# The second layer's down projection as seven block products instead of eight, with the sums of weights made by accumulating DMAs

## The chip, the cores and the metric

The kernel runs on one core of one Trainium2 chip. The metric is the device time of one execution in microseconds; the kernel before has a median of 1347.08 us over 3 runs (1346.73 to 1347.09). TensorE is called PE here, VectorE DVE, ScalarE ACT, GpSimd POOL and SyncE SP.

## What is computed

A decoder trunk of two layers over 512 tokens of width 1024: a Mamba-2 mixer and a ConvFFN, then differential attention and a second ConvFFN. The change touches only the last matrix product of the second ConvFFN:

```python
def conv_ffn(x, ln_g, up_w, conv_w, conv_b, down_w):
    u = causal_dwconv(rms_norm(x, ln_g) @ up_w, conv_w, conv_b)
    gate, up = u[..., :FFN_DIM], u[..., FFN_DIM:]
    return (jax.nn.silu(gate) * up) @ down_w
...
    x = x + ff.astype(x.dtype)          # FFN_DIM = 2816, D_MODEL = 1024, SEQ = 512
```

All arrays are float32.

## The kernel before

Every product of float32 operands is made from three matmuls in a fast type: each operand is split into a high part (rounded to float32r by ACT) and a low part (the rest, by DVE), and high times high, high times low and low times high are added in PSUM.

**Weights.** All weights of the program stand in one list, `plan`, in the order in which PE uses them, cut into chunks of 128 partitions by 1024 columns (512 KB). For each chunk `emit_chunk` writes one DMA on SP's queue into a buffer `wr` (three buffers), one ACT instruction that makes `wh` (L147) and one DVE instruction that makes `wl` (L158). `wh` and `wl` have three buffers each. `chunk(key)` hands out the next chunk and emits those up to two places ahead of it.

**The second ConvFFN** (`ffn(1, ...)`) goes over 22 blocks of 128 features, called pairs here since each has a gate and an up product. For a pair, PE makes `ps_g` and `ps_u` (24 matmuls of 128x128 by 128x512 each, `mm3`, L204 to L206), DVE scales them (L931), ACT and DVE make the three taps of the convolution (L932, L934), ACT applies Silu (L995), DVE multiplies gate and up (L1001), and the product is split into `hh` (ACT, L1002) and `hl` (DVE, L1003). The 22 pairs are cut in two parts, 12 and 10. After each part comes its share of the down projection, `down_tokens`: for each half c of the 1024 output columns, four PSUM banks (one for each block of 128 tokens) collect all features of the part. The stationary operand is a block of `hh` or `hl` (features by tokens), the moving one 512 columns of `wh` or `wl` (L970 to L972). At the end of each half, DVE adds the four banks to the residual `xr` (L977, or L983 in the last part, where the halves of 256 columns are stored at once). The last two feature blocks of the very last bank are made in two halves of 256 columns (`end`), so that the last addition is short.

The program is written through a layer that puts the instructions of each engine in an order of its own and sets the waits between them; what that order is for the two kernels is shown below.

Of the kernel before, what the change touches and what calls it, by code (L numbers as in the profile page):

```python
# [18 lines left out]
P = 128  # L19
T = 512  # L20
D = 1024
KB = D // P
NT = T // P
# [5 lines left out]
FFN = 2816  # L29
NPAIR = FFN // P  # L30
HALF = 12
AH = 8
EPS = 1e-6
NEG = -1.0e30
# [5 lines left out]
def trunk_kernel(ctx: ExitStack, tc, x, ssm_ln_g, ssm_in_w, ssm_conv_w, ssm_conv_b, ssm_dt_bias,  # L40
# [46 lines left out]
    out_chunks(NG - 1)  # L87

    def ffn_plan(l):
        for h, (p0, p1) in enumerate(((0, HALF), (HALF, NPAIR))):  # L90
# [97 lines left out]
    def emit_chunk():  # L188
        i = state["next"]
        if i < len(plan):  # L190
            state["next"] = i + 1
            with tc.issue_after(state["rs"]) if i < 5 else nullcontext():
# [715 lines left out]
    def ffn(l, norm, bp, gnext, nnext):  # L908
        with tc.tile_pool(name="ffn_h%d" % l, bufs=1) as hp, tc.tile_pool(name="ffn%d" % l, bufs=1) as fp:
# [13 lines left out]
            def taps(j, p, ps):  # L923
                key = "%s%d_%d" % ("gu"[j], l, p)
                r = rr[0]
                col = lambda t: cf[l][:, 88 * j + 22 * t + p:88 * j + 22 * t + p + 1]
                u = fp.tile([P, T], F32, tag="u", name="u" + key, bufs=3)
                v = fp.tile([P, T], F32, tag="v%d" % j, name="v" + key, bufs=3)
# [3 lines left out]
                act.activation(v, u, AF.Identity, bias=col(3), scale=col(2))  # L932
                for s in range(1, 3):
                    dve.scalar_tensor_tensor(out=v[:, s:], in0=u[:, :T - s], scalar=col(2 - s),  # L934
                                             in1=v[:, s:], op0=ALU.mult, op1=ALU.add)
                return v
# [13 lines left out]
            def down_tokens(p0, n, hh, hl, last):  # L950
                for c in range(2):
                    cols = slice(c * 512, (c + 1) * 512)
                    pss = [mm_bank("ps_d%d_%d_%d" % (p0, c, b)) for b in range(NT)]
                    for k0 in range(0, n, 2):
                        wh, wl = chunk("d%d_%d_%d" % (l, c, p0 + k0))
                        for b in range(NT):
                            ts = slice(b * P, (b + 1) * P)
                            if last and c == 1 and b == NT - 1 and k0 + 2 == n:
                                end = [aux_bank("end%d" % j) for j in range(2)]
                                for j in range(2):  # L960
                                    for k in range(k0, k0 + 2):
                                        h, w = (t[:, k - k0, j * 256:(j + 1) * 256] for t in (wh, wl))
                                        o = end[j][:, :256]
                                        pe.matmul(o, hh[k][:, ts], h, start=k == k0, stop=False)
                                        pe.matmul(o, hh[k][:, ts], w, start=False, stop=False)
                                        pe.matmul(o, hl[k][:, ts], h, start=False, stop=k == n - 1)
                                continue
                            stop = n - 3 if last and c == 1 and b == NT - 1 else n - 1
                            for k in range(k0, k0 + 2):
                                pe.matmul(pss[b], hh[k][:, ts], wh[:, k - k0, :], start=k == 0, stop=False)  # L970
                                pe.matmul(pss[b], hh[k][:, ts], wl[:, k - k0, :], start=False, stop=False)  # L971
                                pe.matmul(pss[b], hl[k][:, ts], wh[:, k - k0, :], start=False, stop=k == stop)  # L972
                            if stop < n - 1 and k0 + 4 == n:
                                dve.tensor_tensor(out=xr[:, b, cols], in0=pss[b], in1=xr[:, b, cols], op=ALU.add)
                    for b in range(NT):
                        if not last:
                            dve.tensor_tensor(out=xr[:, b, cols], in0=pss[b], in1=xr[:, b, cols], op=ALU.add)  # L977
                            continue
                        ended = c == 1 and b == NT - 1
                        for j in range(2):  # L980
                            h = slice(j * 256, (j + 1) * 256)
                            x_ = xr[:, b, c * 512 + j * 256:c * 512 + (j + 1) * 256]
                            dve.tensor_tensor(out=x_, in0=end[j][:, :256] if ended else pss[b][:, h], in1=x_, op=ALU.add)  # L983
                            (act if j != ended else sync).dma_start(
                                out[0, b * P:(b + 1) * P, c * 512 + j * 256:c * 512 + (j + 1) * 256], x_)

            for p0, p1 in ((0, HALF), (HALF, NPAIR)):
                last = p1 == NPAIR
                hh, hl = [], []
                for p in range(p0, p1):  # L990
                    ps = [products(0, p)]
# [6 lines left out]
                    up = taps(1, p, ps[1])  # L998
                    h = hp.tile([P, T], F32R, tag="hh", name="hh%d_%d" % (l, p), bufs=HALF + 1)
                    w = hp.tile([P, T], F32R, tag="hl", name="hl%d_%d" % (l, p), bufs=HALF + 1)  # L1000
                    dve.tensor_tensor(out=ga, in0=ga, in1=up, op=ALU.mult)  # L1001
                    act.activation(h, ga, AF.Copy)  # L1002
                    dve.tensor_tensor(out=w, in0=ga, in1=h.bitcast(F32), op=ALU.subtract)  # L1003
                    hh.append(h)
                    hl.append(w)
                n = p1 - p0
                if nnext is None:
                    down_tokens(p0, n, hh, hl, last)
# [382 lines left out]
```

## Time and profile before

| | |
|---|---|
| median of 3 runs | 1347.08 us (1346.73 to 1347.09) |
| the profiled execution's own time | 1346.85 us |
| its span, first to last instruction | 1345.2 us |
| granted TensorE clock | 1.0 throughout |
| second ConvFFN's first matmul | 977.8 us |
| first share of its down projection | 1113.0 to about 1178.3 us |
| second share | about 1287 to 1341.8 us |

The busy time of an engine is the sum of its instructions' durations. PE's matmuls overlap each other, so PE's busy time says that PE always had one in flight, and the spacing of their starts says how fast it goes. A group of instructions is given by its line, engine and tiles, with its busy time, the mean of one, and the idle time before it with what ended it.

### The profile page before, as it was taken

The page shows a single profiled execution, that of the slowest core. Times are in us where ns is not written, and L with a number is a line of the kernel's source. Part 1 is how long each engine was busy: PE and PEld are TensorE (multiplying, and loading weights), DVE is VectorE, ACT ScalarE, POOL GpSimd, SP SyncE. Part 2 cuts the span into 40 slices and gives each one's busy share as a digit, 9 for nine tenths or more (in the row PEclk, how much of TensorE's full clock was granted, in tenths as well). Part 3 has the DMA queues.
Part 4 walks back from the last instruction along what each step waited for, and adds up shares of the span by engine and source line. Part 5 has one row for each costly group of instructions (what it writes and reads, how often), then busy time and mean ns, then how long its engine had stood idle before and what let it go on. Part 6 is the DMA issues. An engine that isn't in the chain of part 4 may idle for free.

```text
span 1345.2 us, 16977 instructions
## 1 busy us (share of the span) xinstructions
PE 1339.8 (100%) x6461; PEld 1099.9 (82%) x6461; DVE 919.6 (68%) x1540; ACT 644.4 (48%) x1062; POOL 100.3 (7%) x139
## 2 busy tenths in 40 slices
PE   9999999999999999999999999999999999999998
PEld 8878888888888888888888887777888888888887
DVE  7889788788877774367754556778777773367743
ACT  6695653652444442134433556777654442134420
POOL 5330401200110000000002100000100000000000
PEclk9999999999999999999999999999999999999999
DMA  7553433432333332333323422221233333333332
GB/s 205 161 149 95 149 95 116 127 95 70 95 94 95 102 101 94 95 95 99 97 79 109 127 79 93 70 80 49 63 94 94 95 94 94 96 105 97 95 94 78
DMA packets 179826, 135.00 MB, mean 100 GB/s; under 512 B 6492, under 2 KB 163552, under 8 KB 179744
## 3 DMA queue, kind: packets, MB, share of 16 engines
q1 hardware_dynamic: 173872, 120.73, 30.5%
q0 software_dynamic: 4592, 12.08, 2.9%
q8 instruction: 51, 0.84, 0.3%
q10 hardware_dynamic: 1280, 1.10, 0.2%
q14 instruction: 31, 0.25, 0.1%
HBM read 131.64 MB, written 2.25 MB: 100 GB/s over the span
## 4 chain that ended last, share of the span: by engine, by line
PE 97%; DVE 1%; ACT 1%; DMA 0%; issue 0%; SPq 0%
PE ps_g L205 6%; PE ps_u L206 6%; PE ps_g L206 6%; PE ps_u L205 6%; PE ps_u L204 6%; PE ps_g L204 6%; PE ps_in L204 5%; PE ps_in L206 5%; PE ps_in L205 5%; PE ps_d L206 3%; PE ps_d L205 3%; PE ps_d L204 3%; PE ps_d L971 3%; PE ps_d L970 3%; PE ps_d L972 3%; PE ps_o L206 2%
## 5 line engine op out<-in xcount | busy, mean ns | idle before, releaser
L204 PE MATMUL ps_u<-xgh,wh_u 128*128 128x512 f32 x352 | 137.4, 390 | 0.0
L205 PE MATMUL ps_g<-xgl,wh_g 128*128 128x512 f32 x352 | 137.1, 389 | 0.0
L204 PE MATMUL ps_g<-xgh,wh_g 128*128 128x512 f32 x352 | 137.0, 389 | 0.0
L206 PE MATMUL ps_u<-xgh,wl_u 128*128 128x512 f32 x352 | 137.0, 389 | 0.0
L206 PE MATMUL ps_g<-xgh,wl_g 128*128 128x512 f32 x352 | 137.0, 389 | 0.0
L205 PE MATMUL ps_u<-xgl,wh_u 128*128 128x512 f32 x352 | 136.9, 389 | 0.0
L204 PE MATMUL ps_in<-xgh,wh_in 128*128 128x512 f32 x304 | 126.0, 414 | 0.0
L158 DVE TENSOR_TENSOR wl_d<-wr_d,wh_d 128x1024 fp32r<-128x1024 f32 (+1 forms) x46 | 54.2, 1179 | 96.9 <-ACT wh_d L147 96.7
L206 PE MATMUL ps_in<-xgh,wl_in 128*128 128x512 f32 x304 | 119.7, 394 | 0.0
L205 PE MATMUL ps_in<-xgl,wh_in 128*128 128x512 f32 x304 | 119.2, 392 | 0.0
L147 ACT ACTIVATE wh_d<-wr_d 128x1024 fp32r<-128x1024 f32 (+1 forms) x46 | 47.1, 1025 | 130.3 <-PE ps_d L972 62.4
L931 DVE TENSOR_TENSOR uu<-ps_u,nr_f 128x512 f32<-128x512 f32 x44 | 30.4, 691 | 77.6 <-PE ps_u L206 77.6
L1002 ACT ACTIVATE hh<-vg 128x512 fp32r<-128x512 f32 x44 | 27.8, 632 | 114.9 <-DVE vg L1001 114.9
L205 PEld LDWEIGHTS ps_g<-xgl,wh_g 128*128 128x128 f32 x352 | 66.1, 188 | 13.9 <-DVE xgl L479 0.3
L204 PEld LDWEIGHTS ps_g<-xgh,wh_g 128*128 128x128 f32 x352 | 66.2, 188 | 13.8
L206 PEld LDWEIGHTS ps_u<-xgh,wl_u 128*128 128x128 f32 x352 | 66.2, 188 | 13.7
L205 PEld LDWEIGHTS ps_u<-xgl,wh_u 128*128 128x128 f32 x352 | 66.1, 188 | 13.6
L206 PEld LDWEIGHTS ps_g<-xgh,wl_g 128*128 128x128 f32 x352 | 66.0, 188 | 13.6
L204 PEld LDWEIGHTS ps_u<-xgh,wh_u 128*128 128x128 f32 x352 | 66.0, 188 | 13.5
L147 ACT ACTIVATE wh_g<-wr_g 128x1024 fp32r<-128x1024 f32 x44 | 46.7, 1061 | 50.5 <-PE ps_u L205 31.1
L204 PE MATMUL ps_d<-hh,wh_d 128*128 128x512 f32 x176 | 68.5, 389 | 0.0
L205 PE MATMUL ps_d<-hl,wh_d 128*128 128x512 f32 x176 | 68.5, 389 | 0.0
(364 smaller groups left out, 3188.2 us busy)
## 6 DMA issues: line engine op xcount, KB each, us to landing
wr_g<-in_ffn_up_w_dram SPq DMA_DIRECT2D x44, 512.0 KB, 3.8
wr_u<-in_ffn_up_w_dram SPq DMA_DIRECT2D x44, 512.0 KB, 3.9
wr_d<-in_ffn_down_w_dram SPq DMA_DIRECT2D x42, 512.0 KB, 3.7
wr_in<-in_ssm_in_w_dram SPq DMA_DIRECT2D x40, 512.0 KB, 4.0
m<-cumd POOLq DMA_DIRECT2D x16, 512.0 KB, 4.9
wr_out<-in_ssm_out_w_dram SPq DMA_DIRECT2D x16, 512.0 KB, 3.5
wr_k<-in_kv_w_dram SPq DMA_DIRECT2D x8, 512.0 KB, 3.9
wr_q<-in_q_w_dram SPq DMA_DIRECT2D x8, 512.0 KB, 3.8
```

The costliest lines, as they stand in the source:

```text
L147: return act.activation(self.wh[:, :self.n], self.raw[:, :self.n], AF.Copy)
L158: return eng.tensor_tensor(out=self.wl[:, :self.n], in0=self.raw[:, :self.n], in1=self.wh[:, :self.n].bitcast(F32), op=ALU.subtract)
L204: pe.matmul(ps, wh, xh, start=start, stop=False)
L205: pe.matmul(ps, wh, xl, start=False, stop=False)
L206: return pe.matmul(ps, wl, xh, start=False, stop=stop).ins
L931: dve.tensor_tensor(out=u, in0=ps, in1=r, op=ALU.mult)
L970: pe.matmul(pss[b], hh[k][:, ts], wh[:, k - k0, :], start=k == 0, stop=False)
L971: pe.matmul(pss[b], hh[k][:, ts], wl[:, k - k0, :], start=False, stop=False)
L972: pe.matmul(pss[b], hl[k][:, ts], wh[:, k - k0, :], start=False, stop=k == stop)
L1002: act.activation(h, ga, AF.Copy)
```

## The change

The features of a part are taken in twos (even and odd block), the tokens in two halves of 256, the output columns in two halves of 512. That makes the down projection of a part a product of 2x2 blocks with 2x2 blocks, and Strassen's scheme in Winograd's form makes it from seven block products instead of eight. They are made in the order 1, 2, 5, 7, 6, 3, 4 (`SEVEN`).

- **Left operands.** For each two pairs, DVE makes four sums of 128x256 (`sums`, L1011) of the activations, and the seven left operands (three of them plain) are split into `sh` and `sl` (L1014, L1015), in place of `hh` and `hl` of two pairs.
- **Right operands.** `z` is first W00 (product 1), then W01 is added in place (product 5), then W11 (product 6), then W10 (product 4). `x` is W01 + W11 (product 7), `y` is W11 (3), and product 2 reads W10. Each addition is a DMA issued from POOL with `accum_op=ALU.add`, from the weights in DRAM onto the tile in SBUF, once the tile has been split for the product before. `z`, `x` and `y` have two tiles of 128x1024 each, for up to four of a part's twos; `x` and `y` lie in the memory of `xT`, whose last readers are the transposes of `residual`. `ahead` loads `z`, `x` and `y` of a part while its third pair is made; `combine` stands in the place of `Weights.split` in the list of chunks.
- **Results.** Each product has two banks (two blocks of 128 tokens). DVE adds them to `xr`, partly through a running sum `run_sum`: 22 instructions of 128x512 a part, and ACT makes 2 copies.
- **Parts.** The 22 pairs are cut in three parts, 8, 8 and 6 (`PARTS_D`).

```diff
+PARTS_D = (0, 8), (8, 16), (16, 22)
+SEVEN = "1257634"
...
             if l == 1:
-                for c in range(2):
-                    for k in range(p0, p1, 2):
-                        plan.append(("d%d_%d_%d" % (l, c, k), *w_cols(ffn_down_w[l], k, 2, c * 512, 512)))
+                for m in SEVEN:
+                    for q0 in range(0, (p1 - p0) // 2, 2):
+                        plan.append(("s%s_%d_%d" % (m, p0, q0), (m, p0, q0, min(2, (p1 - p0) // 2 - q0))))
                 continue
...
+            def plus(t, p0, q0, nq, j, i):
+                pool.dma_start(view(t, nq), source(p0, q0, nq, j, i), accum_op=ALU.add)
+            def ahead(p0, n):
+                for q0 in range(0, n // 2, 2):
+                    c, nq = q0 // 2, min(2, n // 2 - q0)
+                    for k, j, i in ("z", 0, 0), ("x", 0, 1), ("y", 1, 1):
+                        sync.dma_start(view(raws[k][c], nq), source(p0, q0, nq, j, i))
+                    plus(raws["x"][c], p0, q0, nq, 1, 1)
+            def combine(key, m, p0, q0, nq):
+                c, n = q0 // 2, nq * 512
+                if m == "2":
+                    t = wrp.tile([P, 1024], F32, tag="raw", name="wr_" + key)
+                    sync.dma_start(view(t, nq), source(p0, q0, nq, 1, 0))
+                else:
+                    t = raws["x" if m == "7" else "y" if m == "3" else "z"][c]
...
+                act.activation(wh[:, :n], t[:, :n], AF.Copy)
+                dve.tensor_tensor(out=wl[:, :n], in0=t[:, :n], in1=wh[:, :n].bitcast(F32), op=ALU.subtract)
+                ready.append((key, view(wh, nq), view(wl, nq)))
+                if m in "156":
+                    plus(t, p0, q0, nq, *{"1": (0, 1), "5": (1, 1), "6": (1, 0)}[m])
...
+                def products(m, b, qs, ps, cols=slice(0, 512)):
+                    for q in qs:
+                        h, w = (t[:, side[m], b * P:(b + 1) * P] for t in sides[q][:2])
+                        wh, wl = ws[q]
+                        pe.matmul(ps, h, wh[:, cols], start=q == qs[0], stop=False)
+                        pe.matmul(ps, h, wl[:, cols], start=False, stop=False)
+                        pe.matmul(ps, w, wh[:, cols], start=False, stop=q == qs[-1])
...
+                        elif m == "6":
+                            add(r, pss[b])
+                            add(to(b, 512), r, ALU.subtract)
+                            add(r, seven[b])
+                            add(to(2 + b, 512), r, ALU.subtract)
+                            add(to(2 + b, 0), r)
...
+                    if cut:
+                        stores((2,), 0)
+                        products(m, 1, range(nq - 1), pss[1])
+                        add(to(3, 0), pss[1])
+                        for j in range(2):
+                            end = aux_bank("end%d" % j)[:, :256]
+                            products(m, 1, [nq - 1], end, slice(256 * j, 256 * (j + 1)))
+                            add(to(3, 256 * j, 256), end)
+                            store(3, 256 * j, act if j else sync)
```

How the instructions stand on DVE in the last share of the down projection, before (the first number of `wl_d1_1_12` says column half 1, the second the feature block; `ps_d12_0_0` is the bank of half 0, token block 0):

```order
L158 TENSOR_TENSOR wl_d1_0_20_10819<-wr_d1_0_20_10816,wh_d1_0_20_10818 128x1024
L158 TENSOR_TENSOR wl_d1_1_12_10849<-wr_d1_1_12_10846,wh_d1_1_12_10848 128x1024
L158 TENSOR_TENSOR wl_d1_1_14_10879<-wr_d1_1_14_10876,wh_d1_1_14_10878 128x1024
L983 TENSOR_TENSOR xr_8539<-ps_d12_0_0_10752,xr_8539 128x256 x2
L983 TENSOR_TENSOR xr_8539<-ps_d12_0_1_10753,xr_8539 128x256 x2
L983 TENSOR_TENSOR xr_8539<-ps_d12_0_2_10754,xr_8539 128x256 x2
L983 TENSOR_TENSOR xr_8539<-ps_d12_0_3_10755,xr_8539 128x256 x2
L158 TENSOR_TENSOR wl_d1_1_16_10929<-wr_d1_1_16_10926,wh_d1_1_16_10928 128x1024
```

The same engine in the last share after the change, from the low part of product 6's first chunk (`wl_s6_16_0`: product 6, part from pair 16, first two twos) to that of product 4's second chunk:

```order
L985 TENSOR_TENSOR wl_s6_16_0_11107<-wz0_8540,wh_s6_16_0_11106 128x1024
L985 TENSOR_TENSOR wl_s6_16_2_11112<-wz1_8541,wh_s6_16_2_11111 128x512
L985 TENSOR_TENSOR wl_s3_16_0_11137<-xT_85,wh_s3_16_0_11136 128x1024
L1031 TENSOR_TENSOR run_sum_8542<-run_sum_8542,ps_s6_16_0_11134 128x512
L1031 TENSOR_TENSOR xr_8539<-xr_8539,run_sum_8542 128x512
L1031 TENSOR_TENSOR run_sum_8542<-run_sum_8542,ps_s7_16_0_11104 128x512
L985 TENSOR_TENSOR wl_s3_16_2_11141<-xT_85,wh_s3_16_2_11140 128x512
L1031 TENSOR_TENSOR xr_8539<-xr_8539,run_sum_8542 128x512 x2
L1031 TENSOR_TENSOR run_sum_8542<-run_sum_8542,ps_s6_16_1_11135 128x512
L985 TENSOR_TENSOR wl_s4_16_0_11179<-wz0_8540,wh_s4_16_0_11178 128x1024
L1031 TENSOR_TENSOR xr_8539<-xr_8539,run_sum_8542 128x512
L985 TENSOR_TENSOR wl_s4_16_2_11183<-wz1_8541,wh_s4_16_2_11182 128x512
```

Where additions of whole banks stood in groups of four between five or six splits, they now stand between the splits of nearly every product, and the splits of products 6 and 4 read `wz0` and `wz1`, which a DMA has changed since the product before.

On POOL, before the change, the last DMAs are two for the attention's bias table, and what follows them to the end is a row of sums for the norm ahead of the second ConvFFN:

```order
L1044 COPY bv0_6173<-rb_6170 8x80
L1044 COPY bv1_6193<-rb_6170 8x320
L1045 DMA bd_6171<-bv0_6173 8x320 [waits Pool_49]
L1045 DMA bd_6171<-bv1_6193 8x320 [waits Pool_49]
L550 TENSOR_TENSOR nacc_f1_6163<-nacc_f1_6163,nsq_f11_8408 128x512 [waits DVE_49,PE_49,Activation_49]
L550 TENSOR_TENSOR nacc_f1_6163<-nacc_f1_6163,nsq_f12_8420 128x512 [waits Activation_49,Pool_49]
```

After it, the accumulating DMAs follow them, in this order for the first part (`xT_85` is the memory in which `x` and `y` lie; a `DMAHW` semaphore is that of a load on SP's queue, a `DMASW` semaphore that of an earlier DMA of POOL, `DVE_49` that of DVE):

```order
L964 DMA wz0_8540<-in_ffn_down_w_dram 128x2x512 [waits DMAHW3_49,DMAHW1_49,DMAHW5_49,DMASW2_49,DMAHW7_49,DMASW1_49,DVE_49]
L964 DMA wz1_8541<-in_ffn_down_w_dram 128x2x512 [waits DVE_49]
L964 DMA wz0_8540<-in_ffn_down_w_dram 128x2x512 [waits DMASW5_49,DVE_49]
L964 DMA wz1_8541<-in_ffn_down_w_dram 128x2x512 [waits DMASW6_49,DVE_49]
L964 DMA xT_85<-in_ffn_down_w_dram 128x2x512 [waits DMAHW6_49,DVE_49]
L964 DMA wz0_8540<-in_ffn_down_w_dram 128x2x512 [waits DMASW7_49,DVE_49]
L964 DMA xT_85<-in_ffn_down_w_dram 128x2x512 [waits DMAHW7_49,DMASW3_49]
L964 DMA wz1_8541<-in_ffn_down_w_dram 128x2x512 [waits DMASW4_49,DMASW0_49,DVE_49]
```

POOL's queue had nothing in this stage and now has eight DMAs a part; two of them, for the next part's `x`, stand between the additions to `z` for product 4.

More of the change, by code (lines that the diff above doesn't have):

```diff
@@ L89, in ffn_plan @@
     def ffn_plan(l):
-        for h, (p0, p1) in enumerate(((0, HALF), (HALF, NPAIR))):
+        for p0, p1 in PARTS_D if l else ((0, HALF), (HALF, NPAIR)):
             for p in range(p0, p1):
@@ L927, in taps @@
                 u = fp.tile([P, T], F32, tag="u", name="u" + key, bufs=3)
-                v = fp.tile([P, T], F32, tag="v%d" % j, name="v" + key, bufs=3)
+                v = fp.tile([P, T], F32, tag="v%d" % j, name="v" + key, bufs=3 if j or nnext is not None else 4)
                 if nnext is None and key in ("g1_1", "u1_1"):
@@ L948, in residual @@
                         act.activation(xr[:, b, c * 512:(c + 1) * 512], pt, AF.Copy)
[L950 to L979, printed above, removed]
-                        for j in range(2):
[L981 to L985, printed above, removed]
@@ L987, in ffn, with source, view @@
-            for p0, p1 in ((0, HALF), (HALF, NPAIR)):
+            raws = {}
+            def source(p0, q0, nq, j, i):
+                src = ffn_down_w[l][(p0 + 2 * q0) * P:(p0 + 2 * q0 + 2 * nq) * P, i * 512:(i + 1) * 512]
+                return src.rearrange("(k j p) c -> j p k c", j=2, p=P)[j]
+            def view(t, nq):
+                return t[:, :nq * 512].rearrange("p (k c) -> p k c", k=nq)
+            def plus(t, p0, q0, nq, j, i):
+                pool.dma_start(view(t, nq), source(p0, q0, nq, j, i), accum_op=ALU.add)
@@ new lines, in ffn, with operands @@
+            if nnext is None:
+                raws["z"] = [fp.tile([P, 1024], F32, name="wz%d" % c) for c in range(2)]
+                for i, k in enumerate("xy"):
+                    raws[k] = [xTt[:, 4 * i + 2 * c:4 * i + 2 * c + 2, :].rearrange("p k t -> p (k t)")
+                               for c in range(2)]
+                state["combine"] = combine
+                run_sum = fp.tile([P, 2, T], F32, name="run_sum")
+            def operands(p, ga, sides):
+                h = ga.rearrange("p (i t) -> p i t", i=2)
+                if p % 2 == 0:
+                    sh = hp.tile([P, 7, 256], F32R, tag="sh", name="sh%d" % p, bufs=4)
+                    sl = hp.tile([P, 7, 256], F32R, tag="sl", name="sl%d" % p, bufs=4)
+                    sides.append((sh, sl, h))
+                    parts = [(slice(0, 1), h[:, 0:1, :])]
+                else:
+                    sh, sl, e = sides[-1]
+                    s = fp.tile([P, 4, 256], F32, tag="sums", name="sums%d" % p, bufs=1)
+                    for o, a, b, op in ((0, e[:, 1], h[:, 1], ALU.subtract), (1, s[:, 0], e[:, 0], ALU.subtract),
+                                        (2, e[:, 0], e[:, 1], ALU.subtract), (3, h[:, 0], s[:, 1], ALU.add)):
+                        dve.tensor_tensor(out=s[:, o], in0=a, in1=b, op=op)
+                    parts = [(slice(3, 7), s), (slice(1, 3), h)]
+                for o, v in parts:
+                    act.activation(sh[:, o], v, AF.Copy)
+                    dve.tensor_tensor(out=sl[:, o], in0=v, in1=sh[:, o].bitcast(F32), op=ALU.subtract)
@@ new lines, in down_tokens, with add, to, store @@
+            def down_tokens(p0, n, sides, last):
+                nq = n // 2
+                side = {"1": 0, "2": 1, "4": 2, "5": 3, "6": 4, "7": 5, "3": 6}
+                def products(m, b, qs, ps, cols=slice(0, 512)):
[5 more added lines that the diff above has]
+                        pe.matmul(ps, w, wh[:, cols], start=False, stop=q == qs[-1])
+                def add(t, v, op=ALU.add):
+                    dve.tensor_tensor(out=t, in0=t, in1=v, op=op)
+                def to(b, c, n=512):
+                    return xr[:, b, c:c + n]
+                def store(b, c, eng):
+                    eng.dma_start(out[0, b * P:(b + 1) * P, c:c + 256], to(b, c, 256))
+                def stores(bs, c):
+                    for b in bs:
+                        for j in range(2):
+                            store(b, c + 256 * j, sync if j else act)
+                for m in SEVEN:
+                    pss = [(aux_bank if m in "273" else mm_bank)("ps_s%s_%d_%d" % (m, p0, b)) for b in range(2)]
+                    cut = last and m == "4"
+                    ws = {}
+                    for q0 in range(0, nq, 2):
+                        wh, wl = chunk("s%s_%d_%d" % (m, p0, q0))
+                        for q in range(q0, min(nq, q0 + 2)):
+                            ws[q] = wh[:, q - q0, :], wl[:, q - q0, :]
+                    for b in range(2):
+                        if not (cut and b):
+                            products(m, b, range(nq), pss[b])
+                    for b in range(2):
+                        r = run_sum[:, b, :]
+                        if m == "1":
+                            add(to(b, 0), pss[b])
+                            act.activation(r, pss[b], AF.Copy)
+                        elif m == "2":
+                            add(to(b, 0), pss[b])
+                        elif m == "5":
+                            add(to(b, 512), pss[b])
+                            add(to(2 + b, 512), pss[b])
+                        elif m == "7":
+                            seven = pss
+                        elif m == "6":
[4 more added lines that the diff above has]
+                            add(to(2 + b, 0), r)
+                        elif m == "3":
+                            add(to(b, 512), pss[b])
+                        elif not (cut and b):
+                            add(to(2 + b, 0), pss[b])
+                    if last and m in "263":
+                        stores((2, 3) if m == "6" else (0, 1), 0 if m == "2" else 512)
+                    if cut:
[7 more added lines that the diff above has]
+                            store(3, 256 * j, act if j else sync)
@@ L988, in ffn @@
+            for p0, p1 in PARTS_D if nnext is None else ((0, HALF), (HALF, NPAIR)):
                 last = p1 == NPAIR
-                hh, hl = [], []
+                hh, hl, sides = [], [], []
                 for p in range(p0, p1):
+                    if nnext is None and p == p0 + 2:
+                        ahead(p0, p1 - p0)
                     ps = [products(0, p)]
@@ L998, in ffn @@
                     up = taps(1, p, ps[1])
+                    if nnext is None:
+                        dve.tensor_tensor(out=ga, in0=ga, in1=up, op=ALU.mult)
+                        operands(p, ga, sides)
+                        continue
                     h = hp.tile([P, T], F32R, tag="hh", name="hh%d_%d" % (l, p), bufs=HALF + 1)
@@ L1007, in ffn @@
                 if nnext is None:
-                    down_tokens(p0, n, hh, hl, last)
+                    down_tokens(p0, n, sides, last)
                     continue
```

5 lines of the change are left out of this document (added).

## The prediction

> **What bounds the kernel now.** I read the page first, then the chain of waits, then windows and groups of the second ConvFFN.
>
> ```profile
> span 1345.2 us, 16977 instructions
> PE 1339.8 (100%) x6461; PEld 1099.9 (82%) x6461; DVE 919.6 (68%) x1540; ACT 644.4 (48%) x1062; POOL 100.3 (7%) x139
> DVE  7889788788877774367754556778777773367743
> PE 97%; DVE 1%; ACT 1%; DMA 0%; issue 0%; SPq 0%
> ```
>
> PE always has a matmul in flight, and the chain that ended last is PE for 97% of the span. A matmul taken out there is time saved, as long as nothing else becomes late. How much one is worth, the chain of waits says, in the first share of the down projection (start, length, line):
>
> ```profile
> 1113.43 0.23 PE ps_d L971
> ...
> 1117.51 0.23 PE ps_d L971
> ```
>
> These two are six blocks of three matmuls apart: 4.08 us / 18 = 0.2267 us a matmul. The groups of the stage give another number, and it is the wrong one:
>
> ```profile
> L970 PE MATMUL ps_d<-wh_d,hh 128*128 128x512 f32 x96 | 37.3, 389 | 0.0
> L147 ACT ACTIVATE wh_d<-wr_d 128x1024 fp32r<-128x1024 f32 x10 | 10.6, 1061 | 36.5 <-PE ps_d L972 35.5 <-PE ps_u L205 0.9
> L158 DVE TENSOR_TENSOR wl_d<-wr_d,wh_d 128x1024 fp32r<-128x1024 f32 x10 | 12.3, 1226 | 30.9 <-ACT wh_d L147 30.9
> L977 DVE TENSOR_TENSOR xr<-ps_d,xr 128x512 f32<-128x512 f32 x7 | 4.6, 687 | 1.8 <-PE ps_d L972 1.8
> ```
>
> The mean of 389 ns contains the overlap with the next matmul. By it 66 matmuls would be worth 25.7 us, by the spacing 15.0 us. [...]
>
> The other engines' room, by stage (start:end, then busy time of PE, PEld, DVE, ACT, POOL; the rows are the up products of pairs 0 to 11 without the first, the first share of down, the second up, the second down):
>
> ```profile
> 989.90:1113.00 123.10, 123.10 (x561) 102.42 (x560) 89.51 (x113) 60.05 (x77) 0.00 (x0) 1.00 0.32 94
> 1113.00:1178.30 65.30, 65.30 (x289) 54.08 (x289) 22.67 (x24) 14.08 (x14) 0.00 (x0) 1.00 0.33 96
> 1178.30:1287.10 108.80, 108.80 (x481) 90.12 (x480) 76.83 (x96) 47.77 (x59) 0.00 (x0) 1.00 0.33 98
> 1287.10:1341.70 54.60, 54.60 (x247) 45.32 (x245) 19.48 (x29) 9.84 (x10) 0.00 (x0) 1.00 0.26 78
> ```
>
> DVE is busy for 71% of an up stage (76.83 of 108.80) and 35% of a down stage (22.67 of 65.30). In a down stage ACT waits for PE to free a weight buffer, and DVE waits for ACT.
>
> **What the change removes.** Down goes from 4 token blocks x 2 halves x 22 blocks x 3 = 528 matmuls of 512 columns to 7 x 2 x 11 x 3 = 462. 66 x 0.2267 = **-15.0 us**.
>
> **What it adds in the up stages.** Durations not yet shown:
>
> ```profile
> L934 DVE SCALAR_TENSOR_TENSOR vg<-ug,cf,vg 128x511 f32<-128x511 f32 (+1 forms) x24 | 17.9, 748 | 1.4 <-ACT vg L932 1.0
> L1003 DVE TENSOR_TENSOR hl<-vg,hh 128x512 fp32r<-128x512 f32 x11 | 7.6, 693 | 7.8 <-ACT hh L1002 7.8
> L1002 ACT ACTIVATE hh<-vg 128x512 fp32r<-128x512 f32 x11 | 7.0, 633 | 27.1 <-DVE vg L1001 27.1
> L983 DVE TENSOR_TENSOR xr<-ps_d,xr x14: 414/416/425, 1311.3 to 1340.7; 128x256 f32<-128x256 f32 x14
> ```
>
> For two pairs DVE gets four sums of 128x256 (4 x 0.42 = 1.7 us) and splits of 256, 512 and 1024 columns (0.42 + 0.69 + 1.23) for two of 512 (1.39): 2.6 us more in 96 x 0.2267 = 21.8 us. 71% becomes 83%. The four banks for `ps_g`/`ps_u` leave DVE more than 10 us to empty one, so I cost it at nothing; without that cover it would be 11 x 2.6 = 29 us.
>
> **What it adds in the down stages.** Each product reads two chunks for 24 matmuls (5.44 us; 18 and 4.08 us in the last part) where one chunk served 24. DVE now has 14 splits and 22 bank additions a part. Back to back, instructions take a little less than their durations:
>
> ```profile
> 1141.54 1.23 DVE L158 TENSOR_TENSOR wl_d<-wr_d,wh_d 128x1024 fp32r<-128x1024 f32 x1 [4.21 <-ACT wh_d L147]
> 1142.68 1.28 DVE L977 TENSOR_TENSOR xr<-ps_d,xr 128x512 f32<-128x512 f32 x2
> ```
>
> 1.14 us a split, 0.64 an addition: 14 x 1.14 + 22 x 0.64 = 30.0 us of PE's 7 x 5.44 = 38.1; in the last part, whose second chunks have 512 columns (about 0.62), 7 x 1.14 + 7 x 0.62 + 14.1 = 26.4 of 28.6. It fits on average, with the last pair's own work on top, and not at every place. I walked through the order of the rows with these durations, from the end of the last up product (t = 0):
>
> - Parts 1 and 2: product 2 wants the last pair's operands at 7.9, they are just there. DVE then splits product 5's first chunk (8.8 to 10.0), the last pair's sums (to 11.2), adds a bank (to 11.8) and splits product 5's second chunk, which is ready at 13.1 where PE wants it at 12.7. After product 6 five additions a bank (two of them wait for the one before) delay the chunks of 3 and 4 by less than 0.1 us each. Sum: 0.5 and 0.4 us, **+0.9 us**.
> - Last part: product 2 waits 0.55 us for ACT's split of the last pair, products 5 and 7 0.25 us for DVE: **+0.8 us**, before any wait for a DMA.
> - The end: product 6's additions and the late splits of product 4 leave DVE eight additions behind. Before, the last store could go 0.5 us after PE:
>
> ```profile
> 1341.48 0.28 PE L966 MATMUL end<-wh_d,hl 128*128 128x256 f32 x1
> 1341.80 0.42 DVE L983 TENSOR_TENSOR xr<-end,xr 128x256 f32<-128x256 f32 x1 [0.29 <-PE end L966]
> ```
>
> After, by the same walk, DVE is done about 2.3 us behind PE: **+1.8 us**.
>
> **The accumulating DMA** is what the trace does not show. Its nearest rows (KB, median us to landing; then lowest, median, highest of `m`; then packets, MB and share of the span on 16 engines):
>
> ```profile
> m<-cumd POOLq DMA_DIRECT2D x16, 512.0 KB, 4.9
> wr_d<-in_ffn_down_w_dram SPq DMA_DIRECT2D x42, 512.0 KB, 3.7
> DMA to landing us min/median/max: 3.7/4.9/6.1
> q0 software_dynamic: 4592, 12.08, 2.9%
> L674 POOL DMA_DIRECT2D m<-cumd x16: 535/550/560, 54.7 to 240.3; - x16
> ```
>
> A plain 512 KB from POOL lands in 4.9 us. Adding must also read the 512 KB that are there: POOL's queue moved 12.08 MB in 2.9% of 1345.2 = 39 us, 1.7 us for 0.524 MB. So I take A = 4.9 + 1.7 = **6.6 us**. Bounds: 3.7, a plain load from SP; above, 9.8, twice the median, and 12.2, twice the slowest, if reading, adding and writing do not overlap.
>
> What A meets: a tile of `z` is free to add to when DVE has split it, and is wanted two products later. In parts 1 and 2 `wz1` is released at 13.1, and PE wants product 6's second chunk at 23.8, less 1.06 + 1.23 + two handovers for the splits: 8.35 us are free. In the last part DVE has scaling and taps of the last pair, a bank addition, product 2's two chunks, three sums, a bank addition and one more split to do (to 8.0) before product 5's first chunk (to 9.2); `wz0` is released at 9.3. At A = 6.6 the addition lands at 15.9, ACT's high part is done at 17.0 and DVE's low part at 18.3; product 6, which begins at 17.1, wants it one matmul later, at 17.5. It waits 0.8. `wz0` is released again at 18.4, lands at 25.0, and is split at 26.1 and 27.4; product 4 could begin at 26.1 and waits 1.15: **+1.95 us**. So 5.8 us are free here. Each further us costs 2 us there, and beyond 8.35 two more in each of parts 1 and 2, 6 us in all.
>
> POOL's queue holds these DMAs in order; the next part's addition to `x` stands ahead of that for product 4, and waits for a load that SP may only begin when product 7's split is done (t = 15 to 18); with 3.7 us it lands before `wz0` is released at 20.4, so it delays nothing. Behind SP's waits for those loads stand later up weights (from `u1_9`); they are wanted at t = 44 and issued at 38, with 3.7 us enough.
>
> **The sum**, against the profiled execution's 1346.85 us (span 1345.2 and 1.65 around it): -15.0 + 0.9 + 0.8 + 1.95 + 1.8 = -9.5, so 1337.3. The median of the runs lies 0.23 above that execution: **1337.6 us**.
>
> **The rivals.**
>
> 1. *The addition lands late (slower).* If the DMA engines read, add and write one piece after the other, A is 12.2: the last part waits 0.8 + 13.2, parts 1 and 2 0.9 + 4 x 3.85 = 16.3, -15.0 + 14.0 + 16.3 + 1.8 = +17.1: 1364 us. It decides from A = 9.4, where the sum is zero; at 9.8 it is +2.7, 1349.8. For it: the trace has no accumulating DMA, and POOL's landings spread from 3.7 to 6.1 without one. Against it: engines that move 512 KB in 1.7 us have most of those 4.9 us for latency, which pieces in flight share.
> 2. *The POOL queue is held up by DVE.* If writing a DMA's descriptors waits for the running DVE instruction, A is up to 6.6 + 1.23 = 7.8: two waits of 1.2 more, 1340.0 us. Against it: POOL's 16 issues of `m` took 535 to 560 ns each, in a stage (slices 2 to 8 of the page) in which DVE was busy for 70 to 90% of the time. [...]
> 3. *The addition is as fast as a load.* A = 3.7: nothing waits for it, -15.0 + 0.9 + 0.8 + 1.8 = -11.5: 1335.6 us. If half of the walk's small waits and of the late end are not there either, 1333.8.
>
> That the change leaves the matmuls in place can be ruled out by its count.
>
> **How the numbers follow.** The forecast (A from 5.8 to 7.3) has 0.38, rival 2 with its neighbours (7.3 to 8.9) 0.17, rival 3 0.12, a result within 0.2% (2.7 us, what a measurement of this kernel can tell from no change; A from 8.9 to 9.8) 0.08, and rival 1 0.25. Faster is 0.38 + 0.17 + 0.12 = 0.67. The range reaches from rival 3's lower end, 1333, into rival 1 as far as A = 10.7, where the waits are 11.0 and 10.3 us and the sum +8.1: 1355 us. About 0.17 stays outside above, 0.02 below. The likeliest case's own range is 1336 to 1339.5.
>
> **What would show it.** The spacing of matmuls stays 0.227 us, and PE has 63 matmuls of 512 columns and 6 of 256 fewer. Additions `wz` from POOL land in 6 to 7.3 us. PE's gaps stand before products 6 and 4 of the last part, released by a DMA through ACT and DVE; the first two parts have under 1 us each. I am wrong if landings are over 9 us (rival 1), if PE waits for DVE where no DMA is late (the walk), or if gaps appear in up stages (the 83%).

## The result, and the profile after

The changed kernel takes **1350.88 us** (median of six runs, 1349.20 to 1354.03), the kernel before, measured beside it, 1346.93: ratio 1.0032, 95% interval 1.0021 to 1.0042. It is 4 us slower where 9.5 less were forecast. The profiled execution took 1349.2 us, the shortest of the six.

The page of the changed kernel (span; busy time by engine; chain of waits):

```profile
span 1347.4 us, 17057 instructions
...
PE 1331.7 (99%) x6392; PEld 1089.4 (81%) x6392; DVE 994.2 (74%) x1658; ACT 670.2 (50%) x1099; POOL 126.3 (9%) x163
...
PE 89%; DMA 4%; DVE 4%; ACT 2%; issue 1%; POOL 0%; DVEq 0%; POOLq 0%; ACTq 0%
```

Its list of DMAs (POOL's queue with packets, MB and share; the additions to `z` and `x` with KB and median us to landing):

```profile
q0 software_dynamic: 10608, 23.61, 8.1%
...
wz<-in_ffn_down_w_dram POOLq DMA_DIRECT2D x15, 512.0 KB, 6.0
...
xT<-in_ffn_down_w_dram POOLq DMA_DIRECT2D x5, 512.0 KB, 8.3
```

The 69 matmuls are gone (6461 to 6392), and an addition to `z` lands after 6.0 us in the median, where 6.6 were forecast. But the chain, 97% PE before, now goes for 4% through DMAs and 4% through DVE. Where PE stood, its waits show (place, what ended the wait, us in total, times, longest), first in part 1, then in part 2:

```profile
PE ps_s L1026 <- ACT wh_s L984: 4.3, 1, 4.3
PE ps_s L1027 <- DVE wl_s L985: 0.8, 2, 0.5
...
PE ps_s L1026 <- ACT wh_s L984: 2.6, 1, 2.6
PE ps_s L1027 <- DVE wl_s L985: 0.8, 1, 0.8
```

Both long waits are in product 4 (first block of tokens, second chunk), in the parts that were to wait under 1 us each. The last part, where I expected the waits, has 0.7 us. The chain of waits of part 1 leads to the cause (start, length, what):

```profile
1083.38 6.17 DMA xT<-in_ffn_down_w_dram
...
1090.10 1.19 POOL xT L964
1091.29 0.18 POOL wz L964
...
1091.99 0.71 POOL xT L964
1092.69 14.50 DMA wz<-in_ffn_down_w_dram
...
1107.30 1.06 ACT wh_s L984
...
1108.39 1.24 DVE wl_s L985
...
1109.67 0.80 PE ps_s L1027
```

POOL issues four additions in a row: next part's `x`, `wz0`, next part's `x`, `wz1`. The first waits for its plain load, which took 6.17 us where 3.7 were forecast. The last, wanted by product 4, is 14.50 us under way. Their issues (count, ns lowest, median, highest, first and last start) and landings (us, lowest, median, highest), `wz` ahead of `xT`:

```profile
L964 POOL DMA_DIRECT2D wz<-in_ffn_down_w_dram x2: 1687/1978/2269, 1090.8 to 1092.7; - x2
...
DMA to landing us min/median/max: 9.3/11.9/14.5
...
L964 POOL DMA_DIRECT2D xT<-in_ffn_down_w_dram x2: 1190/1481/1772, 1090.1 to 1092.0; - x2
...
DMA to landing us min/median/max: 5.8/8.7/11.7
```

In the order of issue they land at 1090.1 + 5.8 = 1095.9, 1090.8 + 9.3 = 1100.1, 1092.0 + 11.7 = 1103.7 and 1092.7 + 14.5 = 1107.2: steps of 4.2, 3.6 and 3.5 us. That looks like one transfer after the other. In part 2 the same four, issued from 1223.2 to 1226.1, land at 1229.0, 1232.9, 1235.0 and 1238.5: steps of 3.9, 2.1 and 3.5 us; the one behind the short step, the third, has 256 KB.

A second loss stands in the windows around each gap, part 1 and then part 2 (start:end, length, busy time of PE, PEld, DVE, ACT, POOL, granted clock, DMA share, GB/s):

```profile
1100.00:1105.00 5.00, 3.74 (x16) 2.43 (x14) 3.02 (x4) 1.06 (x1) 0.00 (x0) 1.00 1.10 250
1105.00:1109.00 4.00, 0.59 (x1) 0.29 (x1) 0.61 (x1) 1.70 (x2) 0.00 (x0) 0.80 0.71 209
1109.00:1113.00 4.00, 3.54 (x9) 2.68 (x9) 4.00 (x6) 0.31 (x1) 0.00 (x0) 0.50 0.48 129
...
1107.40:1114.20 6.80, 5.33 (x12) 3.89 (x13) 4.76 (x6) 1.91 (x2) 0.00 (x0) 0.50 0.36 102
1240.50:1243.90 3.40, 2.91 (x7) 2.34 (x8) 3.40 (x6) 0.13 (x1) 0.00 (x0) 0.50 0.22 77
```

From 1107.4 us on the granted clock is 0.50, and in the 4 us from 1109 lie 9 matmuls (in an undisturbed window it is 19 or 20). In all it is 0.50 for 6.8 us in part 1 and for 3.4 us in part 2. In the timeline of matmuls:

```profile
1103.66 0.40 PE L1028 MATMUL ps_s<-wh_s,sl 128*128 128x512 f32 x1
1108.41 0.80 PE L1026 MATMUL ps_s<-wh_s,sh 128*128 128x512 f32 x1 [4.35 <-ACT wh_s L984]
1109.67 0.80 PE L1027 MATMUL ps_s<-wl_s,sh 128*128 128x512 f32 x1 [0.46 <-DVE wl_s L985]
1110.26 0.63 PE L1028 MATMUL ps_s<-wh_s,sl 128*128 128x512 f32 x1
1110.69 0.63 PE L1026 MATMUL ps_s<-wh_s,sh 128*128 128x512 f32 x1
...
1115.77 0.40 PE L208 MATMUL ps_g<-xgh,wh_g 128*128 128x512 f32 x1
```

From 1109.67 to the first up matmul stand 17 matmuls: 17 x 0.2267 = 3.85 us would do, they took 6.10, so about 2.25 are lost to the clock. The same reckoning gives 1.48 in part 2 (17 matmuls from 1240.99 to 1246.32), 3.7 us together.

### The profile page after: what moved, and what is told of

It reads as the page before. It is cut to its first block, busy times and chain, and to the rows that moved or that the text cites. A ratio compares the mean times of both kernels' runs of the same rounds, so it can differ in the third digit from the quotient of the medians.

```text
span 1347.4 us, 17057 instructions
## 1 busy us (share of the span) xinstructions
PE 1331.7 (99%) x6392; PEld 1089.4 (81%) x6392; DVE 994.2 (74%) x1658; ACT 670.2 (50%) x1099; POOL 126.3 (9%) x163
## 3 DMA queue, kind: packets, MB, share of 16 engines
q1 hardware_dynamic: 173904, 120.73, 30.3%
q0 software_dynamic: 10608, 23.61, 8.1%
HBM read 143.17 MB, written 2.25 MB: 108 GB/s over the span
## 4 chain that ended last, share of the span: by engine, by line
PE 89%; DMA 4%; DVE 4%; ACT 2%; issue 1%; POOL 0%; DVEq 0%; POOLq 0%; ACTq 0%
PE ps_g L209 6%; PE ps_u L208 6%; PE ps_g L210 6%; PE ps_g L208 6%; PE ps_u L209 6%; PE ps_u L210 6%; PE ps_in L208 5%; PE ps_in L210 5%; PE ps_in L209 5%; PE ps_d L210 3%; PE ps_d L209 3%; PE ps_d L208 3%; DMA wz<-in_ffn_down_w_dram 3%; PE ps_o L210 2%; PE ps_o L208 2%; PE ps_o L209 2%
## 5 line engine op out<-in xcount | busy, mean ns | idle before, releaser
L208 PEld LDWEIGHTS ps_u<-xgh,wh_u 128*128 128x128 f32 x352 | 66.1, 188 | 13.5
L209 PEld LDWEIGHTS ps_u<-xgl,wh_u 128*128 128x128 f32 x352 | 66.1, 188 | 13.5
L1099 ACT ACTIVATE vg<-vg 128x512 f32<-128x512 f32 x44 | 27.8, 633 | 89.8 <-DVE vg L938 89.8
L210 PE MATMUL ps_d<-hh,wl_d 128*128 128x512 f32 x176 | 68.5, 389 | 0.0
L938 DVE SCALAR_TENSOR_TENSOR vu<-uu,cf,vu 128x511 f32<-128x511 f32 x88 | 65.7, 747 | 3.1 <-ACT vu L936 1.7
L938 DVE SCALAR_TENSOR_TENSOR vg<-ug,cf,vg 128x511 f32<-128x511 f32 x88 | 65.8, 747 | 3.0 <-ACT vg L936 1.5
```

Of the source, the lines that this page charges most:

```text
L208: pe.matmul(ps, wh, xh, start=start, stop=False)
L209: pe.matmul(ps, wh, xl, start=False, stop=False)
L210: return pe.matmul(ps, wl, xh, start=False, stop=stop).ins
```

## The experiments

My theory: the next part's transfers, above all its additions to `x`, delay product 4's additions to `z`, and the clock drop behind each gap makes it worse. The rivals: the addition by itself is too slow; the plain loads of the next part fill the DMA engines; DVE's work is the cost. The kernel before was measured again beside the experiments, at 1346.82 us beside the first four below and 1346.63 beside the other three, so their medians can be compared with the 1350.88 of the changed kernel to about 0.3 us.

### The next part's transfers later

```diff
-            def ahead(p0, n):
+            def ahead(p0, n, seen=None):
...
+                        if seen is not None:
+                            act.activation(raws[k][c][:, 0:1], seen[:, 0:1], AF.Copy)
                         sync.dma_start(view(raws[k][c], nq), source(p0, q0, nq, j, i))
...
-                        ahead(p0, p1 - p0)
+                        ahead(p0, p1 - p0, ga if p0 else None)
```

> The next part's loads into the tiles of z, x and y, and the addition to x, are held back until the second pair of the new up stage is done (a write of one column by ScalarE stands ahead of each load); nothing else moves. Theory (the second chunk's addition for product 4 lands after 14.5 and 12.5 us in the first two parts, because the next part's loads and additions share the DMA engines and POOL's queue with it): its landing goes back to 6 to 7 us, the gaps of 4.35 and 2.62 us and the slow matmuls behind them go, 11 to 13 us are won against the changed kernel: about 1339 us (1337 to 1341). Rival 1 (an accumulating transfer of 512 KB is itself too slow in this place): landings stay over 10 us and the time at 1349 to 1351. Rival 2 (the loads only move elsewhere and then hold up the up weights of the third and fourth pair): the gaps of the down stages go, new PE waits come in the up stages, 1343 to 1349.

Measured: **1335.75 us** (1334.49 to 1336.62), ratio to the kernel before 0.9916, interval 0.9903 to 0.9930; 15.1 us less than the changed kernel, more than I expected. The waits of PE over the whole second ConvFFN, and the additions to `z`:

```profile
PE ps_s L1029 <- DVE wl_s L987: 0.3, 1, 0.3
```

```profile
wz<-in_ffn_down_w_dram POOLq DMA_DIRECT2D x15, 512.0 KB, 5.7
...
xT<-in_ffn_down_w_dram POOLq DMA_DIRECT2D x5, 512.0 KB, 9.1
```

Both gaps are gone, and no new wait came in the up stages: rivals 1 and 2 of the expectation fall. For product 4 of part 1 the two additions to `z` land after 5.5 and 5.6 us. The additions to `x` take even longer than before (9.1 us), and nobody waits for them there. The one issued at 1140.02 was late with its queue empty ahead of it:

```profile
L964 POOL DMA_DIRECT2D xT<-in_ffn_down_w_dram x1: 1190/1190/1190, 1140.0 to 1140.0; - x1
...
DMA to landing us min/median/max: 9.3/9.3/9.3
```

Before it POOL had issued nothing since 1092.10. But six plain loads of 512 KB for the next part had been let go on SP's queue (the first of ACT's columns ahead of them is written at 1133.9), and the second load of `x` ended POOL's next wait, at 1144.07, so loads were under way beside the addition for some 4 of its 9.3 us. No run takes those loads away there, so that they delayed it is my estimate.

### Without the additions to x

```diff
-                    plus(raws["x"][c], p0, q0, nq, 1, 1)
+                    if p0 == 0:
+                        plus(raws["x"][c], p0, q0, nq, 1, 1)
```

> Left out: the additions to x for the second and third part (two of 512 KB, one of 512 KB and one of 256 KB); the plain loads of the next part stay as early as they are. This parts POOL's queue and the extra accumulating traffic from the plain loads. If only what stands ahead of it in POOL's queue delays the addition for product 4: all of it comes back, 1338 to 1341. If only the plain loads of SP do it: nothing comes back, 1349 to 1351. I expect most of it, since by the trace the late addition was issued behind an addition to x that had waited 6.98 us for its load, and ran beside it: 1340 to 1344.

Measured: **1336.11 us** (1335.12 to 1336.67), ratio 0.9919 (0.9906 to 0.9933): all of it, not most. The two additions to `z` for product 4 of part 1, and the window in which the second is under way:

```profile
L964 POOL DMA_DIRECT2D wz<-in_ffn_down_w_dram x2: 1203/1203/1203, 1089.7 to 1092.8; - x2
...
DMA to landing us min/median/max: 5.7/6.2/6.7
```

```profile
1093.00:1097.00 4.00, 4.00 (x20) 3.30 (x19) 3.50 (x6) 1.12 (x2) 0.97 (x1) 1.00 1.06 178
```

SP's plain loads are as early as in the changed kernel, the 16 DMA engines are as full there (share 1.06, 1.08 in the changed kernel), and yet the additions land in 5.7 and 6.7 us. The plain loads by themselves are not the cause.

### Without the additions to z

```diff
-                if m in "156":
+                if m in "":
```

> Left out: all additions to z, so that products 5, 6 and 4 read the weights of product 1; the instructions of the other engines stay as they are. This is what the additions cost in all, waits and slow clock included. Theory (matmuls removed are worth 15.0 us, and beside the additions the change costs 0.8 us in the last part and 1.8 at the end): 1334 to 1336. Rival (VectorE's backlog or the two-operand sums cost the time, not the transfers): 1345 and more.

Measured: **1334.25 us** (1333.73 to 1334.86), ratio 0.9907 (0.9892 to 0.9922), as the theory said. DVE's work is the same here, so its backlog and its sums are not the cost. Against the kernel with the late transfers, where the additions to `z` are all made, it gains 1.5 us: so little they cost when nothing stands ahead of them.

### Matmuls to fill the gap

```diff
+                        for _ in range({0: 16, 8: 10}.get(p0, 0) if m == "4" and b == 0 and q == 2 else 0):
+                            pe.matmul(fill, xgh[0][:, :P], xgh[1], start=True, stop=True)
                         pe.matmul(ps, h, wh[:, cols], start=q == qs[0], stop=False)
...
+                    fill = pss[1]
```

> Only added: 16 matmuls of 512 columns in the first part and 10 in the second, with no use for the result, at the place where product 4 waits for its second chunk (3.6 and 2.3 us at 0.227 us each, less than the waits of 4.35 + 0.46 and 2.62 + 0.76 us). Theory (the granted clock falls because TensorE stood still, and 17 matmuls in each part then run at up to 0.43 us instead of 0.227, 2.2 + 1.5 us lost): the clock stays at 1.0, 3 to 4 us come back: 1347 to 1348. Rival (the clock falls for another reason, or the slow spacing is the waiting for weights): no gain, 1350 to 1352.

Measured: **1346.37 us** (1343.11 to 1349.20, eleven runs), ratio 0.9995 (0.9985 to 1.0005): 4.5 us less than the changed kernel for 26 matmuls more, a little more than I expected. The runs of both kernels scatter over 5 or 6 us, so the 4.5 is good to a microsecond or two. The same windows as above:

```profile
1105.00:1109.00 4.00, 3.44 (x14) 2.27 (x13) 0.92 (x1) 2.01 (x2) 0.00 (x0) 1.00 0.70 222
1109.00:1113.00 4.00, 3.64 (x16) 2.99 (x17) 3.84 (x6) 0.77 (x1) 0.00 (x0) 1.00 0.40 131
```

The clock stays at 1.00 where it was 0.80 and 0.50. The waiting for the addition is still there (the late one of part 1 lands after 13.5 us), only the price of having stood still is not. So the clock drop is an effect of the gap, and about 4 us of the loss. In part 1 of the changed kernel PE stood still for 4.35 us, and the clock was 0.50 for 6.8 us. Part 2, with 2.62 and 0.76 us of standing still around one matmul and 3.4 us at 0.50, shows that this single matmul did not hold the clock up.

### Only the order in POOL's queue

```diff
-                pool.dma_start(view(t, nq), source(p0, q0, nq, j, i), accum_op=ALU.add)
+                pin(pool.dma_start(view(t, nq), source(p0, q0, nq, j, i), accum_op=ALU.add))
```

`pin` keeps POOL's additions in the order in which the code makes them. The scheduler had put them as `x`, `wz0`, `x`, `wz1`; now they stand as `wz0`, `wz1`, `x`, `x`. No other engine's order changes.

> Only the order of the additions in POOL's queue changes: in the first two parts those to x come behind both additions to z for product 4 (before: x, z, x, z). All loads and all bytes stay, and the additions to x now run beside the late landings of z. Leaving the additions to x out gave 1336.1 us with the plain loads as early as in the changed kernel, so the plain loads alone cost nothing; open is whether the additions to x hurt by standing ahead in the queue or by running beside. Theory (POOL's queue works its transfers off one after the other): z's additions for product 4 land in 5 to 7 us, 1336 to 1338. Rival (the 16 DMA engines are full and shared): they still take 9 us and more, 1341 to 1348.

Measured: **1336.00 us** (1334.96 to 1336.85), ratio 0.9917 (0.9904 to 0.9931). Landings of `wz`, then of `xT`, and the window in which the changed kernel had its gap:

```profile
L964 POOL DMA_DIRECT2D wz<-in_ffn_down_w_dram x2: 1190/1193/1196, 1090.5 to 1093.7; - x2
...
DMA to landing us min/median/max: 5.5/6.2/6.9
...
L964 POOL DMA_DIRECT2D xT<-in_ffn_down_w_dram x2: 1689/1938/2186, 1094.4 to 1095.1; - x2
...
DMA to landing us min/median/max: 9.4/11.1/12.7
```

```profile
1097.00:1101.00 4.00, 4.00 (x19) 3.18 (x18) 3.96 (x6) 1.59 (x2) 0.30 (x1) 1.00 1.02 234
1101.00:1105.00 4.00, 4.00 (x20) 3.29 (x19) 4.00 (x7) 2.12 (x2) 0.00 (x0) 1.00 1.11 235
```

All transfers are still made, at about the same time, the DMA engines are as full as before (1.02 and 1.11), and the additions to `x` were issued while `wz1`'s was under way. Yet it lands in 6.9 us. The late ones are now those at the end of the queue. So here it is what stands ahead of the addition in POOL's own queue that delays it. What came behind it or ran beside it in this place cost 1.1 to 1.3 us (6.7 and 6.9 us against 5.6 with the late transfers). That is no rule for other places: beside many loads of SP the addition to `x` above took 9.3 us with POOL's queue empty ahead of it. How the queues share the DMA engines, no run shows. That POOL's queue works its additions off in their order agrees with the steps of 2.1 to 4.2 us and with the run without additions to `x`.

### Plain loads in the place of additions

```diff
-                pool.dma_start(view(t, nq), source(p0, q0, nq, j, i), accum_op=ALU.add)
+                pool.dma_start(view(t, nq), source(p0, q0, nq, j, i))
```

> Every addition becomes a plain load of the same block by the same queue in the same order (sums not formed, bytes from the weights the same): what accumulating itself costs. Forecast took 4.9 + 1.7 = 6.6 us for an addition, the 1.7 by bounds. If adding makes a transfer longer by 1 to 2 us: z's loads by POOL land in 4 to 5 us in the median rather than 6.0, the late one of the first part in 9 to 11 rather than 14.5, and the time is 1339 to 1345. If adding costs nothing and only the order in the queue does: landings as they were, 1349 to 1351.

Measured: **1334.27 us** (1334.03 to 1334.87), ratio 0.9907 (0.9893 to 0.9920), less than I expected: nothing is lost, though the order is again `x`, `wz0`, `x`, `wz1`. The last of the four in part 1, which I expected after 9 to 11 us, lands after 5.7. From its list of DMAs:

```profile
q0 software_dynamic: 7792, 23.61, 5.5%
...
wz<-in_ffn_down_w_dram POOLq DMA_DIRECT2D x15, 512.0 KB, 4.1
...
xT<-in_ffn_down_w_dram POOLq DMA_DIRECT2D x5, 512.0 KB, 5.4
```

For the same 23.61 MB the queue was busy for 5.5% of 1332.2 us = 73 us, with additions 8.1% of 1347.4 = 109. The 36 us between them belong to 11.53 MB that were added, the equivalent of 22 transfers of 512 KB: 1.6 us each. A landing takes 4.1 us rather than 6.0. The four are also issued further apart, over 4.0 us rather than 2.6, since the plain load that the first one waits for lands after 4.5 us rather than 6.17. So it takes both, the order and the longer transfers, to make product 4 late.

### The short part first

```diff
-PARTS_D = (0, 8), (8, 16), (16, 22)
+PARTS_D = (0, 6), (6, 14), (14, 22)
```

> The kernel with the late loads (1335.75 us), and the parts cut as 6, 8 and 8 pairs rather than 8, 8 and 6, so that the last part's products take 10.9 us each rather than 8.2. By the changed kernel's trace VectorE ends 1.9 us behind TensorE, and TensorE waits for lower halves in the last part. Theory (a longer last part gives VectorE and the additions time; the first part has then the narrow place, with the loads of the next part kept away): 0.5 to 1.5 us less, 1334.3 to 1335.3. Rival (the short part's waits only move to the front): 1335.5 to 1337.

Measured: **1334.94 us** (1334.57 to 1335.91), ratio 0.9912 (0.9899 to 0.9926). The runs overlap with those of the late transfers (1334.49 to 1336.62), so whether it is better is not decided. The last matmul and DVE's last addition, first with the late transfers, then with the short part first:

```profile
1327.64 0.28 PE L1030 MATMUL end<-wh_s,sl 128*128 128x256 f32 x1
1329.18 0.75 DVE L1033 TENSOR_TENSOR xr<-xr,end 128x256 f32<-128x256 f32 x2
```

```profile
1328.89 0.28 PE L1030 MATMUL end<-wh_s,sl 128*128 128x256 f32 x1
1329.29 0.75 DVE L1033 TENSOR_TENSOR xr<-xr,end 128x256 f32<-128x256 f32 x2
```

DVE ends 0.9 us behind PE instead of 2.0, as hoped, but PE ends 1.25 us later, and the gain is gone. Which small waits took it back I did not follow up. The versions with late transfers, with the new order and with the short part first are all about 11 us faster than the kernel before.

## Why the prediction was wrong

**The step that failed** is the sentence that the next part's addition to `x`, ahead of that for product 4 on POOL, "delays nothing". I asked only when the instruction would be issued. Even that came out late: the load of `x` that it waits for was taken at 3.7 us, and it took 6.17. It ran beside the additions to `z` issued at 1079.05 and 1081.92; in the kernel without additions to `z` a load of `x` takes 3.7 in the median, in the changed kernel 5.8. Still, the issue of `wz1`'s addition moved by little: 1092.69 us in the profile, against 1092.10 in the kernel with late transfers. What I left out is that the transfer itself stands in the queue behind the two additions to `x` and the one to `wz0`. A = 6.6 us was a price for an addition that has the queue to itself, and I used it for one that has three others ahead of it. The change of order alone gave the whole 15 us back, so this is shown. The measured time lies inside the forecast's range of 1333 to 1355 us, but the range reached so far up for rival 1, whose mechanism is not the one that was found; that it holds the time is luck.

**A term that was missing** is the granted clock behind a gap of several us. The prediction took all matmuls at 0.2267 us. By the spacing it is 3.7 us, by the run with the filled gaps 4.5, with the scatter said there.

**The account.** Until the first up matmul of part 2 the changed kernel lost 1115.77 - 1107.07 = 8.7 us against the one with late transfers, 0.3 of it before the down stage. Part 2 took 1246.32 - 1115.77 = 130.55 us instead of 125.27, 5.3 more, and the last part 0.6 more. That is 14.6 us, the difference of the spans (1347.4 and 1332.8). The first up matmuls of parts 2 and 3, first with the late transfers, then that of part 3 in the changed kernel (that of part 2 stands above):

```profile
1107.07 0.39 PE L208 MATMUL ps_g<-xgh,wh_g 128*128 128x512 f32 x1
...
1232.34 0.39 PE L208 MATMUL ps_g<-xgh,wh_g 128*128 128x512 f32 x1
```

```profile
1246.32 0.39 PE L208 MATMUL ps_g<-xgh,wh_g 128*128 128x512 f32 x1
```

**What held:**

- *Fewer matmuls.* 69 fewer, 0.2267 us apart outside the slow stretches. The kernel without additions to `z` shows 12.6 us less than before; the forecast's terms without waits for the additions gave 11.5.
- *The up stages.* In the up stage of part 2 DVE is busy for 47.94 of 59.00 us, 81% where 83% were forecast, and PE never waits:

```profile
1121.00:1180.00 59.00, 59.00 (x262) 48.88 (x261) 47.94 (x65) 27.47 (x35) 0.00 (x0) 1.00 0.34 99
```

- *The addition by itself.* 6.0 us in the median (forecast 6.6), of which 1.6 to 1.9 for adding (forecast 1.7).
- *The end.* DVE was to be done 2.3 us behind PE; in the changed kernel it is 2.0 (PE 1342.26 + 0.28, DVE 1343.81 + 0.75).
- *Only a size was off* in the last part: 1.95 us of waiting for the additions were forecast, and all additions to `z` together cost 1.5 us where nothing stands ahead of them. The small waits of the walk (0.9 and 0.8 us) were hardly there either: with the late transfers PE waits 0.3 us in all.

**The rivals.** Rival 1 has the sign, but not the mechanism: an addition to `z` that has nothing ahead of it in the queue lands in about 6 us, not the 12.2 at which it priced reading, adding and writing one after the other; how these overlap, no run shows. It also put 14.0 of its 30.3 us of waits into the last part, where there was hardly any. Its point of decision, a landing over 9.4 us, was passed in just the two parts where another transfer stood ahead. Rival 2 (POOL held by DVE) is not seen: plain loads took 0.72 us to issue and additions 1.19 beside the same work on DVE. Rival 3's time of 1335.6 us was reached by a kernel that does not wait, though an addition is not as fast as a load. As it stands, the sum -9.5 us is near the version with the other order (1336.0 us, 10.6 less than the kernel before beside it), not the one that was changed.

## What to carry to other kernels

The landing of a DMA is not one number (here the additions to `z` of 512 KB took 5.5 to 14.5 us to product 4): add up what stands ahead of it in its own queue, and price transfers on a queue like instructions on an engine. Then ask what other queues move at the same time (an addition with nothing ahead of it in its queue took 9.3 us beside SP's loads). Where a scheduler orders them by the readiness that it reckons, look up the order in which it put the late one, and hold work for later behind work that is wanted now. And a gap on TensorE can cost more than its length: here the slow clock behind one gap of 4.35 us and one of 2.62 and 0.76 us cost some 4 us on top.

## What the runs showed of the hardware

- In the changed kernel four additions of 512 KB issued within 2.6 us by POOL landed 3.5 to 4.2 us apart, in their order (in part 2 issued within 2.9 us, the third of 256 KB, 2.1 to 3.9 apart). Without the two to `x`, with the DMA share still at 1.06, the other two landed after 5.7 and 6.7 us.
- With the late transfers an addition to `x` with nothing ahead of it in POOL's queue (issued at 1140.02, the one before at 1092.10) landed after 9.3 us, beside SP's plain loads of the next part.
- An addition took POOL 1.19 us to issue, a plain load of the same form 0.72, and an addition directly behind another up to 2.3 us. An addition took more packets (10608 to 7792 for the kernel's whole queue), 1.6 us more of the queue's time per 512 KB, and landed 1.6 to 1.9 us later in the median (5.7 and 6.0 against 4.1).
- The granted clock fell to 0.50 at a gap of 4.35 us, for 6.8 us, and at one of 2.62 and 0.76 us around a single matmul, for 3.4 us. Matmuls without use in the gap kept it at 1.00.
